# Feed-forward weights in one ring for each product, and the queries' low part in both partition halves

## The chip, the cores and the metric

The kernel runs on one NeuronCore of a Trainium2 chip. The metric is the device time of one execution in microseconds (us). TensorE's matmuls appear as PE in the profile, its weight loads as PEld, VectorE as DVE, ScalarE as ACT, GpSimd as POOL and SyncE (which issues nearly all the DMAs) as SP.

## The reference

One layer of a hybrid encoder over 512 positions of width 1024, all in float32:

```
h = rms_norm(x) ; proj = h @ w_in            # 1024 x 7168
merged = sum over 4 branches of sigmoid(gate) * (branch @ its out matrix)
x = x + merged @ w_o
h = rms_norm(x)
up = causal_conv3(h @ w_up)                  # 1024 x 5632, gate half and value half
x = x + (silu(gate) * value) @ w_down        # 2816 x 1024
out = rms_norm(x)
```

Branch B is stick-breaking attention with 4 heads of 64 channels: the scores are z = q.k / 8, and the weight of a key is sigmoid(z) times the product of 1 - sigmoid over the keys between it and the query. The other branches are a gated convolution, an RWKV-7 recurrence and a spatial gating unit; the change does not touch them.

## The kernel before

Each large product is done in three matmuls of the type fp32r: an operand is split in a high part (a rounded copy) and a low part (the remainder), and high x high, high x low and low x high are summed in PSUM. `mm3` (lines 168 to 172) issues the three and calls `tick()`, which lets the side threads (attention, the recurrence) issue some of their own instructions between the large products. TensorE runs in the order in which the program is written; for the other engines a planner orders the instructions.

**Weights.** They come in pieces of 128 x 512 values (256 KB). `load_piece` (line 107) takes three places for a piece: `raw`, into which SP's DMA writes, `whi` and `wlo`. `split` (line 99) makes the high part on ACT (line 100) and the low part on DVE (line 101). In which pool the places lie is told by the list `wslots`, through which the pieces go in turn. Pool `wA` has 4 `raw` and 7 pairs of `whi` and `wlo`. From the product with `w_o` on there is a second pool `wB` with 2 `raw` and 9 pairs, and the list is 7 entries of `wA` followed by 9 of `wB` (line 1021), 16 in a cycle.

**Where the pools lie.** The left side of the on-chip memory is a stack, in bytes of a partition, counted from the sizes of the tiles: constants, `wA` from 23.7 KB (its `whi` and `wlo` from 31.7 to 59.7 KB), the normalised activations h in high and low part (59.7 to 91.7 KB), small tiles, `wB` from 92.8 KB (its `whi` and `wlo` from 96.8 to 132.8 KB), and above it the feed-forward's own pool `fp`, with the high and low parts `aH` (140.8 to 156.8 KB) and `aL` (156.8 to 172.8 KB) of the activated channels, 8 places of 2 KB each. On the right side stand `mgH` (159.0 to 175.0 KB) and `mgL` (175.0 to 191.0 KB), the operands of the product with `w_o`, with 2 KB for each of their 8 row blocks; they are given up before `fp` is opened.

**Feed-forward** (lines 1103 to 1108). The 22 pairs of channel blocks go in groups of 6, 6, 6 and 4. `up_pair(i)` multiplies 4 pieces of `w_up`, as the stationary operand, with h, as the moving one, in 48 matmuls of 512 columns (pair 0 in 96 of 256), each piece serving 12 in a row; then the convolution, the activation and the split follow on ACT and DVE. After the pairs of a group, `row_unit` loads two pieces for each row block of `w_down`, and `tok_gemm` runs the down product: here the activations `aH` and `aL` are stationary and the pieces move. Since the 16 entries go on in turn, pairs 2 and 3 lie in `wB`, pair 4 in `wA`, three pieces of pair 5 in `wA` and one in `wB`; in the first group's down product row blocks 0 to 3 lie in `wB` and 4 and 5 in `wA`. Over the whole feed-forward 600 of the 1008 up matmuls of pairs 1 to 21 read pieces in `wB`, and 258 of the 516 down matmuls of 512 columns read pieces in `wA`.

**Scores** (lines 880 to 933). For each block of two heads the queries' high part is written to both partition halves of `qS` (lines 887 and 888), and the low part to a head's own half of `qL` (line 889). `kS` holds the keys' high part in the head's own half and the low part in the other. For each of 4 key blocks (512, 384, 256 and 128 queries wide) TensorE then multiplies over all 128 partitions with `qS` (line 931), over the own 64 partitions with `qL` (line 932) and adds the mask with a matmul of 128 columns (line 933). That is done for each of 4 heads, between the gate products. The pattern of lines 952 (suffix sums) and 964 (values) is the same two matmuls, high and low, over all 128 partitions.

Of the kernel before, what the change touches and what calls it, by code (L numbers as in the profile page):

```python
# [9 lines left out]
F32 = mybir.dt.float32  # L10
F32R = mybir.dt.float32r
AF = mybir.ActivationFunctionType
ALU = mybir.AluOpType
AX = mybir.AxisListType

P = 128
T = 512
D = 1024
NT = T // P
KT = D // P  # L20
# [6 lines left out]
NEG = -1.0e30  # L27

NRA, NWA = 4, 7
NWB = 9  # L30
NACT = 8

YA, YB, YC, YD, YE, YF, YG, YH = 6, 16, 32, 20, 15, 5, 11, 3
# [15 lines left out]
def hybrid_encoder_layer(  # L49
# [8 lines left out]
    vec, act, pe, pool, sp = nc.vector, nc.scalar, nc.tensor, nc.gpsimd, nc.sync  # L58

    const = ctx.enter_context(tc.tile_pool(name="const", bufs=1))  # L60
    wA = ctx.enter_context(tc.tile_pool(name="wA", bufs=1))
# [5 lines left out]
    def open_pool(name, side="left"):  # L67
        st = ExitStack()
        p = st.enter_context(tc.tile_pool(name=name, bufs=1, side=side, reuse_waits="tile"))
        return p, st  # L70

    def bank(tag="mm"):
        return psum.tile([P, 512], F32, tag=tag, name=tag, bufs=4)
# [25 lines left out]
    def split(src, hi, lo, eng=vec):  # L99
        act.copy(hi, src)  # L100
        eng.tensor_tensor(out=lo, in0=src, in1=hi.bitcast(F32), op=ALU.subtract)  # L101


    wslots = [(wA, NRA, NWA)] * NWA
# [13 lines left out]
    def piece(k, parts):  # L118
        raw_hi_lo, hl = load_piece(k, parts)
        split(*raw_hi_lo)  # L120
        return hl

    def rows_of(w):
        return w.rearrange("(k p) c -> p k c", p=P)
# [4 lines left out]
    def col_unit(w, *cols, get=piece):  # L129

        n = 256 // len(cols)
        return [get(2, [(slice(n * i, n * i + n), w[:, 2 * h:2 * h + 2, c:c + n]) for i, c in enumerate(cols)]) for h in range(w.shape[1] // 2)]

    def row_unit(w, i):

        return [piece(1, [(slice(0, 512), w[:, i:i + 1, 512 * h:512 * h + 512])]) for h in range(2)]
# [25 lines left out]
    def finish(thread, steps=None):  # L162
        while threads.get(thread) and steps != 0:
            threads[thread][0][1] = 0
            step(thread)
            steps = None if steps is None else steps - 1
# [198 lines left out]
    def y_split(br, j, src):  # L365
        tg, nb = {"a": ("yab", 2), "b": ("yab", 2), "c": ("yc", 2), "d": ("yd", 2)}[br]
        y = ypool.tile([P, 2, T], F32R, tag=tg, name="y", bufs=nb)
        yH[br, j], yL[br, j] = y[:, 0, :], y[:, 1, :]
        split(src, yH[br, j], yL[br, j])
# [380 lines left out]
    for j in range(2):  # L750
        ps = pss2[j]
# [5 lines left out]
    for j in range(2):  # L757
        ps = pss2[j]
# [4 lines left out]
    for j in range(2):  # L763
        ps = pss2[j]
# [27 lines left out]
    for tt in range(NT):  # L792
        ps = psg[tt]
# [77 lines left out]
    apool, ast = open_pool("apool", "right")  # L871


    HS = [slice(0, 64), slice(64, P)]
    qS, qL, kS, vS = [], [], [], []

# [4 lines left out]
    for j in range(2):  # L881
        ps = pss2[j]
        qs = apool.tile([P, 2, T], F32R, tag="qS", name="qS", bufs=2)
        ql = apool.tile([P, T], F32R, tag="qL", name="qL", bufs=2)
        for hp in range(2):
            own, oth = HS[hp], HS[1 - hp]
            act.mul(qs[own, hp, :], ps[own, :], 0.125)
            act.mul(qs[oth, hp, :], ps[own, :], 0.125)
            vec.scalar_tensor_tensor(out=ql[own, :], in0=ps[own, :], scalar=0.125, in1=qs[own, hp, :].bitcast(F32), op0=ALU.mult, op1=ALU.subtract)
        qS.append(qs)  # L890
        qL.append(ql)
    pss2 = gemm2(col_unit(w_in_v, SB0 + 256))
    for j in range(2):
        ps = pss2[j]
        ks = apool.tile([P, 2, T], F32R, tag="kS", name="kS", bufs=2)
        for hp in range(2):
            own, oth = HS[hp], HS[1 - hp]
            act.copy(ks[own, hp, :], ps[own, :])
# [3 lines left out]
    for j in range(2):  # L902
        ps = pss2[j]
# [6 lines left out]
        for hp in range(2):  # L910
            own, oth = HS[hp], HS[1 - hp]
            src = pt.rearrange("p (s c) -> p s c", s=4)[:, :, own]
# [6 lines left out]
    def attention():  # L919
        for j in range(2):  # L920
            yt = apool.tile([P, T], F32, tag="yt", name="yt", bufs=2)
            for hp in range(2):
                own, oth = HS[hp], HS[1 - hp]
                zb = [bank("wk"), bank("wk"), bank("wk")]

                def zreg(si, t0=0):
                    b, o = divmod(OFF[si], 512)
                    return zb[b][:, o + t0:o + W[si]]

                for si in range(4):  # L930
                    pe.matmul(zreg(si), lhsT=kS[j][:, hp, si * P:(si + 1) * P], rhs=qS[j][:, hp, si * P:T], start=(si != 3), stop=False)
                    pe.matmul(zreg(si), lhsT=kS[j][own, hp, si * P:(si + 1) * P], rhs=qL[j][own, si * P:T], start=False, stop=False)  # L932
                    pe.matmul(zreg(si)[:, 0:P], lhsT=ident_r, rhs=neg_r, start=False, stop=(si != 1))
                yield Y1
                az = apool.tile([P, 1280], F32, tag="az", name="az", bufs=2)
                spH = apool.tile([P, 1280], F32R, tag="spH", name="spH", bufs=2)
                spL = apool.tile([P, 1280], F32R, tag="spL", name="spL", bufs=2)
                BR = [(0, 512, 512), (512, 1024, 512), (1024, 1280, 256)]
                for b, (a, e, w) in enumerate(BR):
                    act.activation(out=az[:, a:e], in_=zb[b][:, 0:w], func=AF.Abs)  # L940
                act.activation(out=az, in_=az, func=AF.Exp, scale=-1.0)
                act.activation(out=az, in_=az, func=AF.Ln, bias=1.0)
                for b, (a, e, w) in enumerate(BR):
                    vec.scalar_tensor_tensor(out=az[:, a:e], in0=zb[b][:, 0:w], scalar=0.0, in1=az[:, a:e], op0=ALU.max, op1=ALU.add)
                split(az, spH, spL)
                yield YE
                for si in range(4):
                    for sj in range(si, 4):
                        lt = tri_r if sj == si else mones_r
                        reg = zreg(si, (sj - si) * P)  # L950
                        for n, s_ in enumerate((spH, spL)):
                            pe.matmul(reg, lhsT=lt, rhs=s_[:, OFF[sj]:OFF[sj] + W[sj]], start=False, stop=(sj == 3 and n == 1), skip_group_check=True)  # L952
                aH = apool.tile([P, 1280], F32R, tag="spH", name="aH", bufs=2)
                aL = apool.tile([P, 1280], F32R, tag="spL", name="aL", bufs=2)
                for b, (a, e, w) in enumerate(BR):
                    act.activation(out=az[:, a:e], in_=zb[b][:, 0:w], func=AF.Exp)
                for a, e in ((0, 512), (512, 1280)):
                    split(az[:, a:e], aH[:, a:e], aL[:, a:e])
                yield YF
                po = bank("wk")  # L960
                for si in range(4):
                    cols = slice(OFF[si], OFF[si] + W[si])
                    for n, a_ in enumerate((aH, aL)):
                        pe.matmul(po[:, si * P:T], lhsT=vS[j][:, hp, si, :], rhs=a_[:, cols], start=(si == 0 and n == 0), stop=(si == 3 and n == 1))
                act.copy(yt[own, :], po[oth, :])
                vec.tensor_tensor(out=yt[own, :], in0=po[own, :], in1=yt[own, :], op=ALU.add)
            y_split("b", j, yt)

    spawn("rw", attention())
    gates("d", False, False, range(ND, 4))  # L970
    finish("rw1")
# [46 lines left out]
    mst.close()  # L1018
    yst.close()
    wB, wst = open_pool("wB")  # L1020
    wslots[:] = [(wA, NRA, NWA)] * NWA + [(wB, 2, NWB)] * NWB
    n_piece[0] = 0
    gb_ffn = fpool.tile([P, D], F32, tag="gb", name="gb_ffn")
    act.dma_start(out=gb_ffn, in_=ffn_norm_g.broadcast_to([P, D]))
# [40 lines left out]
    def up_pair(i):  # L1065
        u = col_unit(w_up_v, i * P, DFF + i * P)
        pu = gemm2_halves([u], lambda: finish("norm"))[0] if i == 0 else gemm2(u)
        ga = conv(pu[0], i, "ga")
        act.activation(out=ga, in_=ga, func=AF.Silu)
        va = conv(pu[1], FT + i, "va")  # L1070
        vec.tensor_tensor(out=va, in0=va, in1=ga, op=ALU.mult)
        aH[i] = fp.tile([P, T], F32R, tag="aH", name="aH", bufs=NACT)
        aL[i] = fp.tile([P, T], F32R, tag="aL", name="aL", bufs=NACT)
        split(va, aH[i], aL[i])
# [26 lines left out]
        fin_last(tt, hf, 512 * hf, 512 * hf + 512, bk)  # L1101

    GROUPS = [(0, 6), (6, 12), (12, 18), (18, 22)]
    for a, e in GROUPS:
        for i in range(a, e):
            up_pair(i)
        ud = [row_unit(rows_of(w_down[0]), i) for i in range(a, e)]
        tok_gemm(lambda kt: aH[a + kt], lambda kt: aL[a + kt], e - a, ud, 0, *((fin_half, fin_last) if e == FT else (add_x,)))
    fpst.close()
    wst.close()  # L1110
# [31 lines left out]
```

## Time and profile before

| | us |
|---|---|
| median of 3 runs | 884.14 |
| lowest and highest | 883.92, 884.91 |
| the profiled execution | 885.09 |
| its span, first to last instruction | 883.4 |
| busy: PE, PEld | 865.9, 709.8 |
| busy: DVE, ACT | 506.0, 413.2 |

The profiled execution is one run with the hardware profiler on; all rows below are of that run, and 1.69 us of its time lie outside the span. The mean granted clock is 0.992 of full speed. A matmul's duration in the rows overlaps that of the next one, since matmuls are pipelined; what one costs is read from one start to the next.

### The profile page before, as it was taken

The numbers are of one execution on the slowest core, as the hardware profiler recorded it, in microseconds if no ns is written. First come the engines' busy times: TensorE is split into PE (matmuls) and PEld (weight loads), VectorE is DVE, ScalarE is ACT, GpSimd is POOL, SyncE is SP. The second block draws the span as 40 slices with busy tenths as digits, with TensorE's granted clock in tenths as the row PEclk, the third lists the DMA queues.
The fourth block names the chain that finished last, engine by engine and source line by source line (L and its number), as shares of the span: only waits on it lengthen the run. The fifth ranks groups of instructions, "written<-read, shape, count | busy, mean of one in ns | idle before, by whom it ended". The sixth has DMA issues, their size and how long they took to land.

```text
span 883.4 us, 12631 instructions
## 1 busy us (share of the span) xinstructions
PE 865.9 (98%) x4767; PEld 709.8 (80%) x4767; DVE 506.0 (57%) x868; ACT 413.2 (47%) x676; POOL 18.9 (2%) x61
## 2 busy tenths in 40 slices
PE   6999999999999999999999999999999999999997
PEld 6978877788778788888888898888888888888876
DVE  5577747875364555544554676634665366634645
ACT  7473345643344587765344554413443144413425
POOL 6000000000000000000000000000000000000000
PEclk9999999999999999999999999999999999999999
DMA  7223331233133322226336252314432063314102
GB/s 242 63 83 99 86 97 49 63 87 97 52 86 93 99 62 65 73 62 200 96 96 182 69 167 96 96 37 117 134 96 84 8 183 107 96 37 131 36 1 95
DMA packets 102773, 82.20 MB, mean 93 GB/s; under 512 B 12716, under 2 KB 92152, under 8 KB 102712
## 3 DMA queue, kind: packets, MB, share of 16 engines
q1 hardware_dynamic: 102040, 79.82, 30.4%
q10 hardware_dynamic: 592, 1.31, 0.5%
q8 instruction: 37, 0.61, 0.3%
q0 software_dynamic: 80, 0.26, 0.1%
q14 instruction: 24, 0.20, 0.1%
HBM read 78.88 MB, written 2.49 MB: 92 GB/s over the span
## 4 chain that ended last, share of the span: by engine, by line
PE 87%; DMA 5%; DVE 4%; ACT 2%; issue 1%; SPq 1%; POOL 0%; ACTq 0%; DVEq 0%
PE mm L169 24%; PE mm L170 24%; PE mm L171 24%; PE wk L169 2%; PE wk L171 2%; PE wk L170 2%; PE wk L552 1%; PE wk L952 1%; DMA raw<-in_w_o_dram 1%; DMA raw<-in_w_in_dram 1%; DMA raw<-in_w_up_dram 1%; DVE wlo L101 1%; DMA x<-in_x_dram 1%; ACT whi L100 1%; PE wk L932 1%
## 5 line engine op out<-in xcount | busy, mean ns | idle before, releaser
L100 ACT CAST whi<-raw 128x512 fp32r<-128x512 f32 x276 | 169.1, 620 | 305.0 <-PE mm L170 148.3
L101 DVE TENSOR_TENSOR wlo<-raw,whi 128x512 fp32r<-128x512 f32 x272 | 185.4, 688 | 172.2 <-ACT whi L100 168.9
L169 PE MATMUL mm<-hH,whi 128*128 128x512 f32 (+1 forms) x448 | 174.3, 389 | 0.9 <-ACT hH L100 0.9
L171 PE MATMUL mm<-hH,wlo 128*128 128x512 f32 (+1 forms) x448 | 169.9, 379 | 3.6 <-POOL wlo L101 3.6
L170 PE MATMUL mm<-hL,whi 128*128 128x512 f32 (+1 forms) x448 | 169.7, 379 | 1.0 <-DVE hL L101 0.9
L170 PE MATMUL mm<-h2L,whi 128*128 128x512 f32 (+1 forms) x368 | 141.0, 383 | 0.5 <-DVE h2L L101 0.5
L169 PE MATMUL mm<-h2H,whi 128*128 128x512 f32 (+1 forms) x368 | 141.2, 384 | 0.1
L171 PE MATMUL mm<-h2H,wlo 128*128 128x512 f32 (+1 forms) x368 | 140.9, 383 | 0.0
L171 PEld LDWEIGHTS mm<-hH,wlo 128*128 128x128 f32 x448 | 85.9, 192 | 19.6 <-POOL wlo L101 3.8
L169 PEld LDWEIGHTS mm<-hH,whi 128*128 128x128 f32 x448 | 85.9, 192 | 18.2 <-issue 1.5
L170 PEld LDWEIGHTS mm<-hL,whi 128*128 128x128 f32 x448 | 85.9, 192 | 15.1 <-DVE hL L101 1.4
L170 PEld LDWEIGHTS mm<-h2L,whi 128*128 128x128 f32 x368 | 69.3, 188 | 14.8 <-DVE h2L L101 0.7
L169 PEld LDWEIGHTS mm<-h2H,whi 128*128 128x128 f32 x368 | 69.3, 188 | 14.5 <-ACT h2H L100 0.3
L171 PEld LDWEIGHTS mm<-h2H,wlo 128*128 128x128 f32 x368 | 69.3, 188 | 14.2
L171 PE MATMUL mm<-whi,aL 128*128 128x512 f32 (+1 forms) x92 | 35.8, 389 | 0.0
L169 PE MATMUL mm<-whi,aH 128*128 128x512 f32 (+1 forms) x92 | 35.7, 388 | 0.0
L170 PE MATMUL mm<-wlo,aH 128*128 128x512 f32 (+1 forms) x92 | 35.7, 388 | 0.0
L169 PE MATMUL wk<-whi,aH 128*128 128x512 f32 (+1 forms) x88 | 34.1, 388 | 0.0
L171 PE MATMUL wk<-whi,aL 128*128 128x512 f32 (+1 forms) x88 | 34.1, 387 | 0.0
L170 PE MATMUL wk<-wlo,aH 128*128 128x512 f32 (+1 forms) x88 | 34.1, 387 | 0.0
L1061 DVE SCALAR_TENSOR_TENSOR ga<-mm,vecs,ga 128x511 f32<-128x511 f32 x22 | 16.5, 749 | 26.4 <-ACT ga L1060 26.4
L1060 ACT ACTIVATE ga<-mm,vecs 128x512 f32<-128x512 f32 x22 | 15.1, 688 | 26.5 <-PE mm L171 26.5
(347 smaller groups left out, 1196.4 us busy)
## 6 DMA issues: line engine op xcount, KB each, us to landing
raw<-in_w_in_dram SPq DMA_DIRECT2D x104, 256.0 KB
raw<-in_w_up_dram SPq DMA_DIRECT2D x176, 128.0 KB
raw<-in_w_down_dram SPq DMA_DIRECT2D x44, 256.0 KB
raw<-in_w_o_dram SPq DMA_DIRECT2D x16, 256.0 KB
x<-in_x_dram SPq DMA_DIRECT2D x4, 512.0 KB
raw<-in_w_in_dram SPq DMA_DIRECT2D x16, 128.0 KB
xt<-in_x_dram SPq DMA_DIRECT2D x4, 512.0 KB
out_dram<-xn SPq DMA_DIRECT2D x4, 320.0 KB
```

Of the source, the lines that this page charges most:

```text
L100: act.copy(hi, src)
L101: eng.tensor_tensor(out=lo, in0=src, in1=hi.bitcast(F32), op=ALU.subtract)
L169: pe.matmul(ps, lhsT=sh, rhs=mh, start=first, stop=False)
L170: pe.matmul(ps, lhsT=sh, rhs=ml, start=False, stop=False)
L171: pe.matmul(ps, lhsT=sl, rhs=mh, start=False, stop=last)
L552: pe.matmul(ps[us, i * 64:i * 64 + 64], lhsT=lt, rhs=rh, start=True, stop=True)
L932: pe.matmul(zreg(si), lhsT=kS[j][own, hp, si * P:(si + 1) * P], rhs=qL[j][own, si * P:T], start=False, stop=False)
L952: pe.matmul(reg, lhsT=lt, rhs=s_[:, OFF[sj]:OFF[sj] + W[sj]], start=False, stop=(sj == 3 and n == 1), skip_group_check=True)
L1060: act.activation(out=t0, in_=ps, func=AF.Copy, scale=ffc(2, i))
L1061: vec.scalar_tensor_tensor(out=t0[:, 1:T], in0=ps[:, 0:T - 1], scalar=ffc(1, i), in1=t0[:, 1:T], op0=ALU.mult, op1=ALU.add)
```

## The change

It has two parts. For the feed-forward, `wslots` is set anew ahead of each product: pieces of `w_up` take places in `wA` alone (7), those of `w_down` in `wB` alone, which now has 4 `raw` and 12 pairs. The row blocks of `w_down` are loaded in between the pairs of the group, from the second pair on (in a group of 6: two after pair 1, one after pair 2, two after pair 3, one after pair 4; in the last group two after pair 1 and two after pair 2), not after the last one. The product with `w_o` keeps its places, 7 in `wA` and 9 in `wB`. By the sizes, `wB`'s `whi` and `wlo` then lie from 100.8 to 148.8 KB, `aH` from 156.8 to 172.8 KB and `aL` from 172.8 to 188.8 KB; `wA` and h stay where they are. For the scores, the queries' low part is written to both halves, by 8 DVE instructions in place of 4, and the second matmul runs over all 128 partitions, so that the product of the two low parts is added as well.

```diff
-NWB = 9
+NRB, NWB = 4, 12
...
-        ql = apool.tile([P, T], F32R, tag="qL", name="qL", bufs=2)
+        ql = apool.tile([P, 2, T], F32R, tag="qL", name="qL", bufs=2)
         for hp in range(2):
             own, oth = HS[hp], HS[1 - hp]
-            act.mul(qs[own, hp, :], ps[own, :], 0.125)
-            act.mul(qs[oth, hp, :], ps[own, :], 0.125)
-            vec.scalar_tensor_tensor(out=ql[own, :], in0=ps[own, :], ...)
+            for to in (own, oth):
+                act.mul(qs[to, hp, :], ps[own, :], 0.125)
+                vec.scalar_tensor_tensor(out=ql[to, hp, :], in0=ps[own, :], ...)
...
-                    pe.matmul(zreg(si), lhsT=kS[j][own, hp, si * P:(si + 1) * P], rhs=qL[j][own, si * P:T], start=False, stop=False)
+                    pe.matmul(zreg(si), lhsT=kS[j][:, hp, si * P:(si + 1) * P], rhs=qL[j][:, hp, si * P:T], start=False, stop=False)
...
-    wslots[:] = [(wA, NRA, NWA)] * NWA + [(wB, 2, NWB)] * NWB
+    inA, inB = (wA, NRA, NWA), (wB, NRB, NWB)
+    wslots[:] = [inA] * NWA + [inB] * (2 * KT - NWA)
...
     for a, e in GROUPS:
-        for i in range(a, e):
-            up_pair(i)
-        ud = [row_unit(rows_of(w_down[0]), i) for i in range(a, e)]
+        n, ud = e - a, []
+        for i in range(n):
+            wslots[:] = [inA]
+            up_pair(a + i)
+            wslots[:] = [inB]
+            while i and len(ud) < n and len(ud) * (n - 2) < n * i:
+                ud.append(row_unit(rows_of(w_down[0]), a + len(ud)))
```

## Rows read from the trace of the kernel before

**Rows 1.** The page: busy time by engine, and the chain that ended last.

```profile
PE 865.9 (98%) x4767; PEld 709.8 (80%) x4767; DVE 506.0 (57%) x868; ACT 413.2 (47%) x676; POOL 18.9 (2%) x61
...
PE 87%; DMA 5%; DVE 4%; ACT 2%; issue 1%; SPq 1%; POOL 0%; ACTq 0%; DVEq 0%
```

**Rows 2.** Waits of PE, whole span, the longest: who, for whom, us, times, longest.

```profile
PE mm L171 <- POOL wlo L101: 3.6, 1, 3.6
```

**Rows 3.** Timeline, PE, first head's scores: start, us, engine, line, operation, tiles, form.

```profile
308.46 0.39 PE L931 MATMUL wk<-qS,kS 128*128 128x512 f32 x1
308.78 0.50 PE L932 MATMUL wk<-qL,kS 64*128 64x512 f32 x1
309.21 0.33 PE L933 MATMUL wk<-neg_r,ident_r 128*128 128x128 f32 x1
309.37 0.39 PE L931 MATMUL wk<-qS,kS 128*128 128x384 f32 x1
```

**Rows 4.** Windows, four heads' scores (308.46, 331.40, 354.39, 377.42 on): their sum.

```profile
sum 12.62, PE 12.62 PEld 7.54 DVE 3.96 ACT 6.70 POOL 0.00; mean PE 3.15 PEld 1.89 DVE 0.99 ACT 1.67 POOL 0.00
```

**Rows 5.** Timeline, PEld, the same scores: the load for line 932.

```profile
308.77 0.18 PEld L932 LDWEIGHTS wk<-qL,kS 64*128 64x128 f32 x1 [0.36 <-issue]
```

**Rows 6.** Timeline, PE: end of a line 952 run, the eight of line 964.

```profile
325.07 0.27 PE L952 MATMUL wk<-spL,mones_r 128*128 128x128 f32 x1
325.18 0.39 PE L952 MATMUL wk<-spH,tri_r 128*128 128x384 f32 x1
...
330.18 0.39 PE L964 MATMUL wk<-aH,vS 128*128 128x512 f32 x1
...
331.40 0.44 PE L931 MATMUL wk<-qS,kS 128*128 128x512 f32 x1
```

**Rows 7.** Timeline, PE: first matmul of up pairs 2, 4 and 5.

```profile
534.05 0.39 PE L169 MATMUL mm<-h2H,whi 128*128 128x512 f32 x1
...
556.37 0.39 PE L169 MATMUL mm<-h2H,whi 128*128 128x512 f32 x1
...
567.26 0.39 PE L169 MATMUL mm<-h2H,whi 128*128 128x512 f32 x1
```

**Rows 8.** Windows, up pairs 1 to 21: second group's stretch, sum of the four.

```profile
611.25:677.57 66.32, 66.32 (x290) 54.18 (x289) 41.34 (x61) 30.24 (x51) 0.00 (x0) 1.00 0.41 122
...
sum 232.11, PE 232.11 PEld 189.58 DVE 138.94 ACT 101.60 POOL 0.00; mean PE 58.03 PEld 47.40 DVE 34.73 ACT 25.40 POOL 0.00
```

**Rows 9.** Windows, four down products without the last token block: the sum.

```profile
sum 116.49, PE 116.49 PEld 94.56 DVE 52.16 ACT 30.23 POOL 0.00; mean PE 29.12 PEld 23.64 DVE 13.04 ACT 7.56 POOL 0.00
```

**Rows 10.** Timeline, PE, first down product, second token block: three starts.

```profile
587.19 0.39 PE L169 MATMUL wk<-whi,aH 128*128 128x512 f32 x1
...
591.95 0.40 PE L169 MATMUL wk<-whi,aH 128*128 128x512 f32 x1
...
594.75 0.39 PE L169 MATMUL mm<-whi,aH 128*128 128x512 f32 x1
```

**Rows 11.** Timeline, PE, product with w_o, row blocks 4 to 7, first token block.

```profile
484.05 0.39 PE L169 MATMUL mm<-whi,mgH 128*128 128x512 f32 x1
...
489.54 0.39 PE L169 MATMUL wk<-whi,mgH 128*128 128x512 f32 x1
```

**Rows 12.** Waits from 500 us on: ACT's split waiting for a weight's DMA.

```profile
ACT whi L100 <- DMA raw<-in_w_up_dram: 24.6, 22, 3.2
```

**Rows 13.** Groups by line, 611.25 to 677.57 us: the two halves of the split.

```profile
L101 DVE TENSOR_TENSOR wlo<-raw,whi 128x512 fp32r<-128x512 f32 x29 | 19.8, 689 | 19.6 <-ACT whi L100 18.6 <-DMA raw<-in_w_up_dram 1.0
L100 ACT CAST whi<-raw 128x512 fp32r<-128x512 f32 x30 | 18.4, 621 | 28.5 <-PE mm L170 18.3 <-DMA raw<-in_w_up_dram 5.9 <-PE mm L171 2.3
```

**Rows 14.** Line 889's instructions, and timeline of the first head's next step.

```profile
L889 DVE SCALAR_TENSOR_TENSOR qL<-mm,qS x4: 682/689/696, 284.4 to 289.4; 64x512 fp32r<-64x512 f32 x4
...
321.10 1.49 DVE L101 TENSOR_TENSOR spL<-az,spH 128x1280 fp32r<-128x1280 f32 x1 [0.80 <-ACT spH L100]
...
323.97 0.39 PE L952 MATMUL wk<-spH,tri_r 128*128 128x512 f32 x1
```

More of the change, by code (lines that the diff above doesn't have):

```diff
@@ L883, in hybrid_encoder_layer @@
         qs = apool.tile([P, 2, T], F32R, tag="qS", name="qS", bufs=2)
-        ql = apool.tile([P, T], F32R, tag="qL", name="qL", bufs=2)
+        ql = apool.tile([P, 2, T], F32R, tag="qL", name="qL", bufs=2)
         for hp in range(2):
             own, oth = HS[hp], HS[1 - hp]
-            act.mul(qs[own, hp, :], ps[own, :], 0.125)
-            act.mul(qs[oth, hp, :], ps[own, :], 0.125)
-            vec.scalar_tensor_tensor(out=ql[own, :], in0=ps[own, :], scalar=0.125, in1=qs[own, hp, :].bitcast(F32), op0=ALU.mult, op1=ALU.subtract)
+            for to in (own, oth):
+                act.mul(qs[to, hp, :], ps[own, :], 0.125)
+                vec.scalar_tensor_tensor(out=ql[to, hp, :], in0=ps[own, :], scalar=0.125, in1=qs[own, hp, :].bitcast(F32), op0=ALU.mult, op1=ALU.subtract)
         qS.append(qs)
```

## The prediction

> **What bounds the kernel now.** The page comes first: PE is busy for 865.9 us, 98% of the span, and 87% of the chain that ended last is PE [rows 1]. PE's own waits come next: the longest is 3.6 us, once, near the start [rows 2]. So nothing that ACT, DVE or a DMA does sooner is worth anything; the time moves if PE's stream of matmuls becomes shorter, or if PE begins to wait. Busy time doesn't tell how long the stream must be, since a matmul's bar of 0.39 us overlaps the next bar. I therefore read the timeline from start to start, and there two places are slow.
>
> The first is the scores. A matmul of 512 columns over 128 partitions starts at 308.46, the one over 64 partitions 0.32 us later, the mask 0.43 us after that, and the next key block 0.16 us later [rows 3]. The weights for the 64-partition matmul are loaded at 308.77, as it starts and after 0.36 us in which no load ran [rows 5]: that load lies on the path. A head's 12 matmuls take 3.12 to 3.17 us, the four heads 12.62 [rows 4]. In line 964 the eight matmuls have the same widths (512, 512, 384, 384, 256, 256, 128, 128), pairs share their weights too, all use 128 partitions, and they take 331.40 - 330.18 = 1.22 us [rows 6].
>
> The second is the step between matmuls of one shape in the feed-forward. Pairs 2 and 3 (weights in `wB`) take 556.37 - 534.05 = 22.32 us for 96 matmuls, 232.5 ns each; pair 4 (weights in `wA`) takes 10.89 us for 48, 226.9 ns [rows 7]. In the down product it is the other way round: 21 matmuls with weights in `wB` take 4.76 us, 226.7 ns each, and the 12 after them in `wA` 2.80 us, 233.3 ns [rows 10]. So a matmul is some 6 ns shorter where weights and activations lie on the same side: `wA` with h (32 to 92 KB), `wB` with `aH` and `aL` (97 to 173 KB).
>
> **The change part by part.**
>
> *Scores.* What goes is four heads x 3.155 us. What comes is, for each head, the eight matmuls of 128 partitions, 1.22 us by line 964, and four masks of 128 columns. A 128-column matmul that follows another one steps by 325.18 - 325.07 = 0.11 us [rows 6]. That is 1.22 + 0.44 = 1.66 us, 1.50 us less for a head, 6.0 us in all. The bounds: if the mask keeps the 0.16 us that it shows now [rows 3], 16 x 0.05 = 0.8 less is won, 5.2; at the 0.06 us that 128 columns would need at 512 columns in 0.23 (estimated from rows 6), 6.8. I take 6.0, since only the mask is in doubt and the 0.11 us is of a like sequence.
>
> At this place the Trainium skill speaks against the change: "TensorE: Matmul & The Clock Gate", section "Part 2: What happens when you issue a matmul", says that a load's time goes by its columns and the row count doesn't matter, and the section "Why this matters for your kernels" that a K=32 matmul takes as long as a K=128 one. By that rule nothing is won here. The rows differ where the two kinds alternate: 0.43 us against 0.23 for 512 columns.
>
> The four added DVE instructions cost 4 x 0.689 = 2.8 us of DVE [rows 14]. The present ones start by 289.4 and the scores at 308.46 [rows 3], 18 us later, so the two queries-and-keys products hide them; bare they would cost 2.8. They hold the product's two PSUM banks for up to 1.4 us longer each; the next product has two other banks, and 48 matmuls (10.9 us) pass before these are wanted. Behind the scores, the next thing PE needs is ready at 321.10 + 1.49 = 322.59 and used from 323.97 on [rows 14]. The matmuls in between are the same, so that lead of 1.4 us stays, less at most 0.1 because the last of the three score banks is done at the end of the scores as before. Nothing is late next there.
>
> *Up product.* 600 matmuls move from `wB` to `wA`, whose places don't move, nor does h: 600 x (232.5 - 226.9) = 3.4 us. The sum agrees: 232.11 us for 1008 now [rows 8] against 1008 x 0.2269 = 228.7. The bounds are 3.2 and 3.5 by the hundredths of a us in the starts.
>
> *Down product.* The sum now is 116.49 us for 504 matmuls [rows 9]. All in `wB` at 226.7 it would be 114.3; after each change from up to down some 8 matmuls step slowly, 0.2 in all, so 2.0 us would be won. But here both operands move: `aL` to 172.8 to 188.8 KB. The nearest row is the product with `w_o`: weights in `wB`, `mgH` in its upper half (167 to 175 KB), `mgL` at 183 to 191 KB, and 24 matmuls take 5.49 us, 228.9 ns [rows 11]. At that rate for all it would be 115.4, 0.9 won after the changes. `aL`'s upper four of eight places lie in the stretch that `mgL` shows slow, the lower ones at the edge. At the across rate, 233.3, for all it would be 117.6, 1.1 lost. I take 1.3, between the two nearest rows.
>
> The same page of the Trainium skill, section "Step-by-step: what each phase is for", says that TensorE has two independent read ports and that loading the next weights takes no bandwidth from the running matmul. By that the side wouldn't matter, and the feed-forward would gain nothing. The rows show 5.6 ns by the side alone.
>
> *Loads.* The number of DMAs, casts and subtracts is the same. The queues that they move past are SP's and the in-order ACT and DVE: the `w_down` pieces now stand among the pairs. Their places are 12, just a group's pieces, and the earliest is cast after all pieces of the second pair, for which `wA` must have turned over; by then the down product before has ended, and no cast stops in front of a held place. In the second group's up stretch DVE is busy for 41.34 of 66.32 us and already does 29 subtracts [rows 8, 13]; after the change 36 a group less the 7 that fit into `wA` during the down product are also 29. So the load of ACT and DVE there is as before. A place of `wA` is needed again 6 pieces later, 6 x 12 x 0.227 = 16.3 us after it is freed; the refill takes 0.62 + 0.69 us [rows 13] and, at the worst of the waits for a DMA, 3.2 more [rows 12], 4.5 us. That hides it; bare it would cost up to 1.3 us a piece.
>
> *Sum.* 6.0 + 3.4 + 1.3 = 10.7 us. The profiled execution took 885.09 us, 883.4 of it span, and the 1.7 around it don't change: 874.4. The median of the runs, 884.14, is 0.95 lower, so the forecast there is 873.5.
>
> **The rivals.** *The 64 partitions are not the cause*: the 0.16 to 0.2 us by which each score matmul is slow belong to the mask or the bank. Then only the 4.7 us of the feed-forward come: 879.4. For it: the mask, too, is slow, at 0.16. Against it: line 952 changes weights and banks as often and steps by 0.11. (It is what the Trainium skill's rule on rows, named above, would give.)
>
> *The ring changes nothing*: the 5.6 ns belong to something that goes with `wB` by chance, such as which pieces were just written. Then 6.0 alone comes: 878.1. For it: no row has the same place on both sides of a change. Against it: up and down have opposite signs. (The Trainium skill's rule on the two ports, named above, would give this time.)
>
> *The up ring starves*, and the kernel is slower. Seven places serve where 16 rotated. If a refill took longer than 16.3 us, every turn of seven pieces would be late by the excess; 88 pieces are 12.6 turns. At 17.2 us the gain of 10.7 is used up (12.6 x 0.85), at 18 us it is 12.6 x 1.7 = 21.4, and the time 894.9. For it: ACT waits 22 times for a `w_up` DMA already [rows 12], and `w_down` pieces stand ahead in SP's queue. Against it: the worst refill now is a quarter of that.
>
> *New waits eat a part*: the last pairs' activations or a late cast let PE wait 3 to 9 us in all: 876.5 to 883.
>
> **How the numbers follow.** The forecast with its bounds has 0.80: low is 6.8 + 3.5 + 2.0 = 12.3 won, 871.8; high is 5.2 + 3.2 - 1.1 = 7.3, 876.8. The 64 partitions not the cause 0.05, ring without effect 0.06, partial waits 0.05, starving 0.04. The range 871.5 to 878.5 takes in the forecast, the ring without effect and a part of the waits, some 0.88. A measurement of this kernel tells 0.2% (1.8 us) from no change: faster 0.95, same 0.01, slower 0.04.
>
> **What would show it.** Scores: line 932 in the form 128x512, its load one matmul ahead, 1.6 to 1.7 us for a head. Up: 226 to 227 ns in every pair. Down: near 227 where `aL` lies low, and up to 229 where it lies high. PE's waits as now. It would be wrong if up pairs still step by 232, if a head's scores stay above 2.5 us, or if PE waits for a `whi` or `wlo` between 523 and 870 us.

## The result, and the profile after

The changed kernel takes 871.44 us (median of 4 runs, 870.98 to 871.75) against 884.52 for the kernel before beside it (4 runs, 883.92 to 885.52): ratio 0.9851, 95% interval 0.9833 to 0.9868. That is 13.1 us, where 10.7 were forecast; the time lies 0.06 us below the range. The profiled execution took 871.75 us, 870.0 of it span; the time outside the span, 1.7 us, is as before.

The page of the kernel after, busy time by engine and the chain of waits [rows 1]:

```profile
PE 852.2 (98%) x4767; PEld 706.0 (81%) x4767; DVE 510.1 (59%) x872; ACT 414.0 (48%) x676; POOL 18.9 (2%) x61
...
PE 90%; DVE 3%; ACT 2%; DMA 2%; issue 1%; POOL 1%; POOLq 0%; ACTq 0%; SPq 0%
```

PE has the same 4767 matmuls and is busy for 13.7 us less; it is still the bound. The first head's scores, timeline of PE, which answers to [rows 3]:

```profile
307.02 0.39 PE L932 MATMUL wk<-qS,kS 128*128 128x512 f32 x1
307.24 0.39 PE L933 MATMUL wk<-qL,kS 128*128 128x512 f32 x1
307.47 0.22 PE L934 MATMUL wk<-neg_r,ident_r 128*128 128x128 f32 x1
307.53 0.39 PE L932 MATMUL wk<-qS,kS 128*128 128x384 f32 x1
```

and the weight loads of the same matmuls, timeline of PEld [rows 5]:

```profile
307.02 0.19 PEld L933 LDWEIGHTS wk<-qL,kS 128*128 128x128 f32 x1
307.25 0.19 PEld L934 LDWEIGHTS wk<-neg_r,ident_r 128*128 128x128 f32 x1
307.48 0.19 PEld L932 LDWEIGHTS wk<-qS,kS 128*128 128x128 f32 x1
```

(The line numbers of the scores are one higher than before.) The load for the second matmul now begins with the first, 0.22 us ahead of its own matmul; before, it began as its matmul did. The steps are 0.22, 0.23 and 0.06 us; before they were 0.32, 0.43 and 0.16.

The windows of PE and the other engines, one line for each stretch (from, to, us, busy time of PE, PEld, DVE, ACT and POOL, PEclk, DMA share, GB/s): the four heads' scores [rows 4],

```profile
307.02:308.67 1.65, 1.65 (x14) 1.57 (x12) 1.08 (x3) 1.25 (x4) 0.00 (x0) 1.00 0.53 159
...
sum 6.79, PE 6.79 PEld 6.47 DVE 3.29 ACT 5.24 POOL 0.00; mean PE 1.70 PEld 1.62 DVE 0.82 ACT 1.31 POOL 0.00
```

the up pairs 1 to 21 [rows 8],

```profile
602.27:667.56 65.29, 65.29 (x289) 54.06 (x288) 41.00 (x61) 30.18 (x50) 0.00 (x0) 1.00 0.41 120
...
sum 228.54, PE 228.54 PEld 189.21 DVE 137.53 ACT 101.12 POOL 0.00; mean PE 57.13 PEld 47.30 DVE 34.38 ACT 25.28 POOL 0.00
```

and the down products without the last token block [rows 9]:

```profile
569.62:602.27 32.65, 32.65 (x145) 27.04 (x144) 13.82 (x21) 7.24 (x12) 0.00 (x0) 1.00 0.16 52
...
sum 114.63, PE 114.63 PEld 94.47 DVE 51.82 ACT 29.63 POOL 0.00; mean PE 28.66 PEld 23.62 DVE 12.95 ACT 7.41 POOL 0.00
```

So the scores gave 12.62 - 6.79 = 5.83 us, up 232.11 - 228.54 = 3.57, down 116.49 - 114.63 = 1.86: 11.3 us. PE waits for no weight from pair 1 to the end. The spans differ by 13.3 us, so 2 us lie elsewhere. Two stretches of the kernel before tell where, windows around 120 us (the recurrence) and behind the fourth head's scores; the same two in the kernel after stand in a fence of their own:

```profile
119.00:122.50 3.50, 3.50 (x28) 2.95 (x26) 0.15 (x1) 2.37 (x4) 0.00 (x0) 0.67 0.26 75
380.59:384.30 3.71, 3.71 (x11) 2.90 (x12) 0.69 (x1) 3.24 (x4) 0.00 (x0) 0.54 0.00 0
```

```profile
118.00:121.50 3.50, 3.48 (x45) 2.76 (x47) 1.07 (x2) 2.27 (x3) 0.00 (x0) 1.00 0.27 83
373.33:377.00 3.67, 3.67 (x18) 3.04 (x18) 0.69 (x1) 3.62 (x5) 0.00 (x0) 1.00 0.00 0
```

The PEclk column is 0.67 and 0.54 in the kernel before, and 1.00 in the kernel after: for a part of the first two stretches TensorE was granted the lower of its levels, 1.2 GHz, and behind the scores 11 matmuls fill the time that 18 fill after. The page hardly shows it: PE counts as busy throughout, and only the mean granted clock is lower, 0.992 against 0.996.

The table splits the spans at five points: the first score matmul, the first matmul with `w_o`, the first of pair 0 behind them, the first matmul of pair 1 and the last of all (first starts of the timeline; the last 6.2 us are the same in all). The last two columns are two more executions of the kernel before, told of below.

| us | before | after | before again, 1 | before again, 2 |
|---|---|---|---|---|
| up to the scores | 308.46 | 307.02 | 306.50 | 306.34 |
| scores to `w_o` | 153.27 | 146.27 | 152.09 | 152.08 |
| `w_o` | 46.07 | 46.07 | 46.07 | 46.08 |
| to pair 1 | 15.27 | 15.83 | 15.30 | 15.21 |
| pair 1 to the last matmul | 354.09 | 348.65 | 354.07 | 354.06 |
| span | 883.4 | 870.0 | 880.2 | 880.0 |

### The profile page after: what moved, and what is told of

It reads as the page before. It is cut to its first block, busy times and chain, and to the rows that moved or that the text cites. A ratio compares the mean times of both kernels' runs of the same rounds, so it can differ in the third digit from the quotient of the medians.

```text
span 870.0 us, 12669 instructions
## 1 busy us (share of the span) xinstructions
PE 852.2 (98%) x4767; PEld 706.0 (81%) x4767; DVE 510.1 (59%) x872; ACT 414.0 (48%) x676; POOL 18.9 (2%) x61
## 4 chain that ended last, share of the span: by engine, by line
PE 90%; DVE 3%; ACT 2%; DMA 2%; issue 1%; POOL 1%; POOLq 0%; ACTq 0%; SPq 0%
PE mm L169 25%; PE mm L171 24%; PE mm L170 24%; PE wk L171 3%; PE wk L170 3%; PE wk L169 3%; PE wk L552 1%; PE wk L953 1%; PE wk L965 1%; DMA raw<-in_w_down_dram 1%; PE wk L496 1%; ACT sq L181 0%; DVE ib L531 0%; DMA x<-in_x_dram 0%; POOL wlo L101 0%
## 5 line engine op out<-in xcount | busy, mean ns | idle before, releaser
L1031 DVE TENSOR_TENSOR xt<-xt,mm 128x512 f32<-128x512 f32 x16 | 11.0, 688 | 31.7 <-PE mm L171 31.7
```

The lines of the kernel that those rows point to most:

```text
L1031: vec.tensor_tensor(out=xt[:, tt, half_of(hf)], in0=xt[:, tt, half_of(hf)], in1=bk, op=ALU.add)
```

## The experiments

Two theories of the matmul's step in the feed-forward stood against each other. The *side* theory is that of the prediction: what counts is on which side of memory weights and activations lie. The *offset* theory: what counts is the distance of their start addresses. By the sizes of the tiles, the starts modulo 256 bytes (the expectations below still count modulo 2048; why 256 is told with the distances) are, in the kernel before, 160 for `wA` and h, 32 for `wB`, `aH`, `aL` and `y`, 224 for `mgH` and `mgL`. So "same side" and "same remainder" go together there, by chance.

**The scores alone** (the diff's `qL` part on the kernel before).

> The scores' part of the change alone, on the kernel before. Theory: a 64-partition matmul among 128-partition ones exposes its weight load, and the parts add up. In the changed kernel the four heads' scores took 5.7 us less than before, so 878.7 from 884.4; and if the low clock after the fourth head's scores (eight matmuls at 0.43 us in the trace of before, 1.5 us) comes from these scores, 877.2. Rival, the parts don't add up or the gain in the scores is found again as a wait behind them: 880 to 884.

Measured: 876.41 us (876.12 to 877.61; before 884.32), ratio 0.9918 [0.9892, 0.9945]. From the scores to `w_o` it takes 146.27 us, as the whole change does; its feed-forward takes 354.06, as before.

**The rings alone** (the diff's `wslots` part, with the old scores).

> The weight rings alone, scores as before. Theory: 5.4 us less by the steps of the feed-forward in the changed kernel, 879.0 from 884.4, up and down matmuls all near 227 ns, and a step of 0.43 us at the low clock after the fourth head's scores can still be seen (if it goes with the 64-partition matmuls). Rival, the low clock was chance: its 1.5 us come and go from run to run whatever the scores are.

Measured: 879.29 us (876.78 to 882.25), ratio 0.9943 [0.992, 0.9967]; feed-forward 348.65 us, as with the whole change. The medians of the parts add up: 7.9 + 5.0 = 12.9 us, against 13.1. But 7.9 is 2 us more than the scores' own stretch gives, 152.08 - 146.27 = 5.8; the part on the sum comes back to that. Here the low clock came behind the third head; window and timeline of PE:

```profile
354.90:358.10 3.20, 3.20 (x9) 2.49 (x9) 0.69 (x1) 2.86 (x4) 0.00 (x0) 0.52 0.00 0
```

```profile
355.58 0.63 PE L171 MATMUL mm<-hH,wlo 128*128 128x512 f32 x1
356.00 0.63 PE L169 MATMUL mm<-hH,whi 128*128 128x512 f32 x1
```

A step of 0.42 to 0.43 us in place of 0.23, some seven times.

**An unused tile of 896 bytes in the kernel before**, ahead of `wB`: it moves `wB`, `y` and `fp` to `wA`'s remainder, by 128 modulo 256; no ring, no order, no score is changed.

```diff
+    gap = small.tile([P, 224], F32, tag="gap", name="gap", bufs=1)
+    nc.gpsimd.memset(gap[:, 0:1], 0.0)
```

> The kernel before with one thing added: an unused tile of 896 bytes in the pool ahead of the second weight ring, so that the second ring, the activations behind it and the branch outputs y start at the same remainder of 2048 bytes as the first ring and h (1696; it was 800). The rings rotate over both pools as before, so weights lie across from the operand in as many matmuls as before. Side theory (a matmul is longer when its operands lie on different sides): no change, 884.4, pairs 2 and 3 still at 232 ns. Offset theory (it is longer when the starts differ in the remainder): every up and down matmul near 227 ns, 5.4 us less in the feed-forward, and some 1.2 us less in the gate products with y: 877.8.

Measured: 877.23 us (875.26 to 877.45), ratio 0.992 [0.9897, 0.9944]. First matmul of pairs 2, 4 and 5, timeline of PE [rows 7]:

```profile
529.67 0.39 PE L171 MATMUL mm<-h2H,whi 128*128 128x512 f32 x1
...
551.43 0.39 PE L171 MATMUL mm<-h2H,whi 128*128 128x512 f32 x1
...
562.31 0.39 PE L171 MATMUL mm<-h2H,whi 128*128 128x512 f32 x1
```

Pairs 2 and 3 lie in `wB`, across from h, and take 551.43 - 529.67 = 21.76 us, 226.7 ns a matmul; pair 4 in `wA` takes 226.7 too. The feed-forward takes 348.59 us, all that the rings gain. The side theory has fallen: it had no gain here. The products with `y` gain less than was expected, 0.6 us in place of 1.2 (151.44 us from the scores to `w_o`, against 152.08). The product with `w_o` loses 0.5: its operand `mgH` stays, so `wB` comes from a distance of 192 to one of 64. Timeline of PE, the 24 matmuls of [rows 11]:

```profile
479.60 0.40 PE L171 MATMUL mm<-whi,mgH 128*128 128x512 f32 x1
...
485.20 0.40 PE L171 MATMUL wk<-whi,mgH 128*128 128x512 f32 x1
```

They take 5.60 us, 233.3 ns a matmul, where they took 5.49.

**The changed kernel with 1152 bytes ahead of the activations.** `aH` and `aL` stay beside `wB` on one side, and only their remainder moves, by 128.

```diff
+    gap3 = fp.tile([P, 288], F32, tag="gap3", name="gap3")
+    nc.gpsimd.memset(gap3[:, 0:1], 0.0)
```

> The changed kernel with 1152 unused bytes ahead of the activations of the feed-forward, so that each down matmul has both operands on the second ring's side as before, but at remainders of 2048 that differ by 1152, as weights in the first ring and the activations did in the kernel before. Side theory: no change, 871.4, down matmuls at 226.7 ns. Offset theory: down matmuls at 233.4 ns, 504 x 6.7 = 3.4 us more, 874.8; up matmuls stay at 226.7.

Measured: 874.53 us (873.01 to 877.9; before 885.14), ratio 0.988 [0.9861, 0.9898]. Windows of the down products:

```profile
572.60:606.19 33.59, 33.59 (x145) 27.03 (x144) 13.83 (x21) 7.21 (x12) 0.00 (x0) 1.00 0.17 53
...
sum 117.72, PE 117.72 PEld 94.53 DVE 51.87 ACT 29.62 POOL 0.00; mean PE 29.43 PEld 23.63 DVE 12.97 ACT 7.41 POOL 0.00
```

117.72 against 114.63: the 504 matmuls are 6.1 ns longer each, with rings, loads and side unchanged. This is the opposite test, and it agrees.

**Which distances are fast.** Two variants of the changed kernel with gaps between the seven places of `wA`, so that h and `whi` start at seven different distances in each (the second has 96 bytes more behind the last place).

```diff
+    wgap = [0, 128, 64, 32, 16, 8, 8]        # first variant, in values of 4 bytes
+    wgap = [0, 16, 32, 96, 48, 8, 16]        # second variant
...
+                pad = wA.tile([P, wgap[n_A[0]]], F32, tag="gap" + m, name="gap", bufs=1)
```

> The changed kernel with the first ring's seven places moved apart, so that weights and h differ in their remainder of 2048 bytes by 1024, 512, 256, 128, 64, 32 and 0 bytes, place by place (a piece serves 12 up matmuls in a row). If whole steps of some size make the difference, the places with a multiple of it step by 226.7 ns and the others by about 232: for 1024, places 0 and 6 fast; for 512, also place 1; for 256, also place 2. Side theory: all fast.

> The same with 960, 896, 768, 384, 192, 160 and 96 bytes. If multiples of 256 are fast, place 2 alone; if of 128, places 1, 2 and 3; if of 64, also 0 and 4. 896 is the difference with the sign turned that the second ring and h had before, 192 is that of the second ring and the operand of w_o in the kernel before, whose matmuls took 228.9 ns. Side theory: all fast.

They took 877.33 and 881.5 us, one run each. Starts of successive pieces of 12 matmuls, timeline of PE: the first variant's places at distance 256 and 128, then the second's at 768 and 384, each with the start that ends it:

```profile
536.88 0.39 PE L179 MATMUL mm<-h2H,whi 128*128 128x512 f32 x1
...
539.61 0.40 PE L179 MATMUL mm<-h2H,whi 128*128 128x512 f32 x1
...
542.40 0.40 PE L179 MATMUL mm<-h2H,whi 128*128 128x512 f32 x1
```

```profile
538.64 0.39 PE L183 MATMUL mm<-h2H,whi 128*128 128x512 f32 x1
...
541.37 0.40 PE L183 MATMUL mm<-h2H,whi 128*128 128x512 f32 x1
...
544.17 0.39 PE L183 MATMUL mm<-h2H,whi 128*128 128x512 f32 x1
```

2.73 and 2.79 us, 2.73 and 2.80 us. The mean steps over the twelve pieces of each place, in ns:

| distance in bytes (modulo 2048) | step |
|---|---|
| 0, 256, 512, 768, 1024 | 229.1, 227.3, 226.7, 228.4, 226.7 |
| 32, 64, 96, 128, 160, 192 | 233.4, 233.0, 232.8, 232.8, 233.5, 233.2 |
| 384, 896, 960 | 233.0, 233.1, 233.0 |

In the first line, 0 and 768 stand behind a slow place and begin with some slow steps; from the seventh matmul on they step by 227.4 and 227.8. Every multiple of 256 is fast, and nothing else that was tried.

**Alternation or 64 rows.** The kernel before with the scores of a head in three loops: four matmuls over 128 partitions, four over 64, four masks.

```diff
                 for si in range(4):
                     pe.matmul(zreg(si), lhsT=kS[j][:, hp, si * P:(si + 1) * P], ...
+                for si in range(4):
                     pe.matmul(zreg(si), lhsT=kS[j][own, hp, si * P:(si + 1) * P], ...
+                for si in range(4):
                     pe.matmul(zreg(si)[:, 0:P], lhsT=ident_r, ...
```

> The kernel before with the same score matmuls in another order: for each head the four over 128 partitions, then the four over 64, then the four masks. Theory that the alternation costs (a load that changes the number of partitions is not done ahead): 2 changes of shape for a head where there were 8, at 0.16 to 0.2 us each, so some 1.1 us less for a head, 4.4 in all: 880 from 884.4. Theory that 64 partitions are slow by themselves: no change, since the same four matmuls run over 64. Theory that the masks' bank or tile is slow: no change either, or a gain in the mask's steps alone.

Measured: 878.51 us (877.81 to 880.74), ratio 0.9935 [0.9916, 0.9953]. The second head, timeline of PE (rows of four are merged):

```profile
328.42 0.79 PE L931 MATMUL wk<-qS,kS 128*128 128x512 f32 x4
329.14 0.84 PE L933 MATMUL wk<-qL,kS 64*128 64x512 f32 x4
329.91 0.66 PE L935 MATMUL wk<-neg_r,ident_r 128*128 128x128 f32 x4
330.41 0.45 PE L169 MATMUL mm<-hH,whi 128*128 128x512 f32 x1
```

Four matmuls of the same four widths take 0.72 us over 128 partitions and 0.77 over 64. The same instructions as before, with two changes of shape a head in place of eight, take 1.99 us in place of 3.16; the four heads take 4.2 us less, where 4.4 were expected. So it is the change between 64 and 128 rows that costs, and not the 64 rows. That the order of the banks is not it is shown by the kernel after, which keeps the old order and has steps of 0.22, 0.23 and 0.06 us.

**The kernel before, twice more**, to see whether the low clock behind the scores belongs to it.

> The kernel before, looked at once more, for the low clock behind the scores (eight matmuls at 0.43 us after the fourth head's scores in the first trace). Theory that the alternating scores bring it on: it is there again after the third or the fourth head, at 1.2 to 1.5 us, as in the trace with the old scores and the new rings. Rival, chance: it is as likely elsewhere, or in the kernels with scores over 128 partitions, where seven traces show none.

> As the look before, one more time. Both theories expect the same as there; a second look tells a rule from one more chance.

881.98 and 881.71 us; neither has it. Window of the first of them, right behind its fourth head's scores:

```profile
378.50:382.00 3.50, 3.50 (x17) 2.95 (x17) 0.69 (x1) 3.22 (x5) 0.00 (x0) 1.00 0.00 0
```

Over all the traces, it came behind alternating scores in 2 of 5, and behind other scores in 0 of 7. That suggests a link and doesn't settle one.

**Equal remainders in the products with `y` and `w_o` too.** The changed kernel with the 896 bytes, and 1344 bytes ahead of `mgH` on the right side, so that the operands of those products start at equal remainders as well.

```diff
+    gap2 = fpool.tile([P, 336], F32, tag="gap2", name="gap2")
+    nc.gpsimd.memset(gap2[:, 0:1], 0.0)
```

> The changed kernel with the same 896 bytes, and 1344 unused bytes on the right side, so that also the operands of the product with w_o start at the remainder 1696. Side theory: as the changed kernel, 871.4. Offset theory: the gate products with y win some 1.2 us and the product with w_o some 0.9 (192 matmuls from 231.5 to 227 ns): 869.3.

Measured: 868.74 us (868.05 to 870.97; before 884.32), ratio 0.9834 [0.9809, 0.9858]. The first 24 matmuls with `w_o`, timeline of PE, the kernel after and then this one:

```profile
453.29 0.39 PE L169 MATMUL mm<-whi,mgH 128*128 128x512 f32 x1
...
458.87 0.40 PE L169 MATMUL mm<-whi,mgH 128*128 128x512 f32 x1
```

```profile
451.40 0.39 PE L171 MATMUL mm<-whi,mgH 128*128 128x512 f32 x1
...
456.84 0.39 PE L171 MATMUL mm<-whi,mgH 128*128 128x512 f32 x1
```

5.58 us became 5.44, 226.7 ns a matmul. By the traces that is 0.7 us less in the product with `w_o` and 0.65 from the scores to `w_o`. All four runs are below those of the kernel after, but the two intervals overlap, so how much the times gain on it is not shown.

## Why the prediction was right and where it failed

The forecast was 2.1 us too high, by two steps: the down product was sized by the wrong row, and the sum put the time lost at TensorE's lower clock at nothing.

*Scores*: right. 6.0 us were forecast, 5.83 came. The step's reason was nearly right: the load on the path is gone. But it is exposed by the change of row count between neighbours, as the grouped scores show. The prediction set the page "TensorE: Matmul & The Clock Gate" of the Trainium skill (section "Part 2: What happens when you issue a matmul"), by which the row count doesn't matter for the time of a load, against the row of 0.43 us. The loads agree with that rule, 0.18 us for 64 rows [rows 5] and 0.19 for 128; in the grouped run the matmuls of one shape differ little (0.77 against 0.72 us). What the rule doesn't cover is the alternation. The mask, the term in doubt, steps by 0.06 us three times in a head and by 0.11 once; the masks of a head cost 0.29 us in place of 0.44. That is given back by the eight others, 1.42 us in place of 1.22 in three heads, since neither the first (0.28 us) nor those right behind a mask step as in line 964.

*Up*: right in size, 3.57 for 3.4 (just above the bound of 3.5), and that by luck. The reason given, the side, was false: the gap of 896 bytes won the same with the weights across. `wA` and h happen to start at the same remainder; at a distance that is no multiple of 256, places of the same ring step by 233 ns, as the table of distances shows. The second group takes 65.29 us [66.32 in rows 8]. *Loads*: right from pair 1 on; the ring didn't starve. Before that it was not quite free: PE waits in the first pair's product, and "to pair 1" is 0.56 us longer. The chain of waits of the kernel after there (start, us, what):

```profile
502.64 4.80 DMA raw<-in_w_down_dram
507.44 0.02 issue
507.46 0.63 ACT whi L100
508.09 0.02 issue
508.11 0.69 DVE wlo L101
508.81 0.61 DVE h2L L101
...
509.46 0.38 PE mm L170
```

A `w_down` piece's split stands ahead of the split of h on ACT and DVE, and the chain spends 4.80 us on its DMA. The kernels with the rings alone and with the gap ahead of `aH` have the same order and take 14.80 and 14.83 us there, so it depends on when that DMA lands.

*Down*: the step that failed among the parts of the change. It was sized at 1.3 us, between 226.7 ns and the 228.9 of the `w_o` row, because `aL` moves to where `mgL` showed slow; 1.86 came, the 2.0 of its upper bound less 0.14. All of `aL` steps by 226.7 ns, its upper places too. The choice rested on the premise that place in memory counts. What counts is the distance of the start addresses modulo 256 bytes: 32 and 32 for `wB` and both activations, wherever they lie; the `w_o` row, with a distance of 192, was no measure for it.

*Sum*: the step that failed by more, about 2 us of the 2.6 between the forecast and the spans. It took the profiled execution, 885.09 us, as if nothing but the change's parts could differ, and so put what TensorE loses at its lower clock at nothing. That one trace held 1.2 us of low clock behind the fourth head (153.27 against 152.09 and 152.08 from the scores to `w_o`), and the kernel after reached its scores 1.44 us sooner, with a full clock around 120 us, where the instructions are the same. The wait just before, on the tile `Dm`, is shorter too; that makes up for 0.5 us that the kernel after loses near the start. Waits of PE between 105 and 130 us, before and after:

```profile
PE wk L552 <- DVE Dm L541: 2.2, 1, 2.2
```

```profile
PE wk L552 <- DVE Dm L541: 1.7, 1, 1.7
```

With them: 11.3 + 1.2 + 1.4 - 0.6 = 13.3 us, the difference of the two spans. Against the two later executions of the kernel before the spans differ by 10.2 and 10.0 us, close to the forecast, but these two are the shortest on record. The 16 runs of the kernel before that were timed beside the experiments have spans of 880.9 to 885.7 us (median 882.8) at a mean granted clock of 0.990 to 0.994; the four of the kernel after have 869.3 to 870.0 at 0.994 to 0.996. So the 13 us came again, and were not the luck of one trace. Among the 16, the spans are 883.4 to 885.7 us at 0.990 and 880.9 to 882.9 at 0.994, some 0.65 us for each 0.001; by that the 0.003 between the means of the two kernels are worth about 2 us, an estimate from these runs. Whether the change itself raises the clock is not shown: the gap of 896 bytes, with alternating scores, had 0.994 to 0.996, the rings alone 0.989 to 0.993. That cause stays open.

*The rivals*: "the 64 partitions are not the cause" is half true, by the grouped scores, but its time, 879.4, didn't come, as the alternation went too. "The ring changes nothing" is refuted by the rings alone, yet the doubt behind it, that `wB` has something by chance, was the right one. The page "TensorE: Matmul & The Clock Gate" of the Trainium skill also has two independent read ports (section "Step-by-step: what each phase is for"), and the prediction concluded that the place of the operands shouldn't matter. The section says nothing of addresses, and the conclusion fell: the gaps alone made the feed-forward 5.5 us shorter and 3.2 us longer. Starving and new waits cost 0.56 us, once.

## What to carry to other kernels

Before weights are moved about for speed, compute the start address of each matmul's two operands (shown here for fp32r matmuls of 512 columns): a gap of under 1 KB gave here what a new ring and a new order of loading gave. Where a step differs between two places, vary one thing at a time in thought first; here "same side" and "same remainder" were one and the same in every row. Keep matmuls with different row counts in runs, or pad them to one shape, even if that doubles the rows. Where a sum of 10 us is made against one trace, go through its PEclk by windows first: a stretch at the low clock may not be there in the next execution. Compare the granted clock of all the timed runs as well.

## What the runs showed of the hardware that was not expected

- An fp32r matmul of 512 columns steps by 226.7 ns when its moving and stationary operands start a multiple of 256 bytes apart, and by some 233 ns at the other distances tried in the feed-forward. Why 256 is not known. One case lies between: the products with `w_o` that read `wB`, at distance 192, step by 228.9 ns [rows 11]. There, too, addresses set the step, since the same 24 matmuls take 233.3 ns each at distance 64 (the gap of 896 bytes) and 226.7 with equal remainders (the last run); why 192 differs from the 233.2 of the table is open.
- Matmuls over 64 and over 128 partitions in turn step by 0.43 and 0.32 us at 512 columns. In a run of one kind four matmuls of 512 to 128 columns take 0.77 and 0.72 us.
- The granted clock fell to its lower level for about 3 us while PE was busy throughout by its rows, right behind alternating scores (2 of 5 traces). Around 120 us it fell during or just behind PE's wait for `Dm` of 2.2 us (the kernel before), 2.6 and 3.4 us (the grouped scores, the gap ahead of the activations), but not behind waits of 2.4 and 2.5 us in two other variants. The step of 512 columns was 0.43 us there. What decides it was not settled.
